# Hybrid encoder block on one core: the offset of the split gate and up weights inside their tiles varies from unit to unit

## Chip, cores and metric

The kernel runs on one core of one Trainium2 chip. The metric is the device time of one execution in microseconds; the time of a kernel is the median of its runs.

## What is computed

One layer of a bidirectional encoder with 512 tokens of width 2048: two token mixers side by side (global grouped-query attention, and attention in a 2-D neighbourhood), gated and summed, then a SwiGLU channel mixer with 5632 hidden features, all in float32. The change lies in the channel mixer's first half, the products with the gate and the up weights:

```python
h2 = rms_norm(x, norm2_w[l]) * (1.0 + sc2) + sh2
ff = (jax.nn.silu(h2 @ w_ffn_gate[l]) * (h2 @ w_ffn_up[l])) @ w_ffn_down[l]
x = x + g2 * ff
```

Here h2 is 512 x 2048, w_ffn_gate and w_ffn_up are 2048 x 5632, and w_ffn_down is 5632 x 2048.

## The kernel before

**Precision.** Every float32 operand is split into two float32r parts, hi (a copy rounded by ScalarE, ACT) and lo (source minus hi, by VectorE, DVE): `split` at line 117, with the ACT instruction at line 118 and the DVE instruction at line 119. A product is three matmuls into one PSUM bank: stationary hi with moving hi, stationary hi with moving lo, stationary lo with moving hi (`mm3` at line 125, the matmuls at lines 126, 127 and 128). So each matmul has its own weight load (LDWEIGHTS, PEld in the profile).

**Stages.** Until about 1100 us the kernel makes the modulation vectors, the input projection, both attentions and the merged output; there, and in the down projection at the end, a matmul mostly has 512 moving columns. `form2` (line 180) computes w_out and w_down with the weights as the moving operand. After w_out comes the gate and up stage, in two parts:

- Line 922 sets the offset `wbufs["at"]` to 16 elements. The first 512 columns of gate are computed directly (`block`, line 926) while the normalised activations h2 are still being made (transposes at line 839, tiles x, f, a and so on); it has 256 moving columns a matmul.
- The loop at line 975 then goes over 11 groups of 512 hidden features, gate and up in each; the first gate is already there, so 21 times it calls `group7` (line 796). This is a 7-product scheme for 2 x 2 blocks (Winograd's form of Strassen). `group7` takes 4 slices of 512 input features one after the other; one slice of one weight matrix, 512 x 512, is a *unit*. For each unit `wforms` (line 775) loads the weights in two transfers (line 133, from SP's queue), forms four differences on DVE (lines 785 to 788, into tiles ta and tb), and splits all into four pairs of tiles, whi and wlo.

**Order of work in a unit.** A unit has 7 products, in the order 1, 2, 3, 5, 6, 7, 4 (`ORDER`, line 756). Product 1 uses the first pair of tiles, products 2 and 3 the second, 5 and 6 the third, 7 and 4 the fourth. Each product has 2 x 2 blocks of 128 x 128 weights and each block has the three matmuls of `mm3`, so a unit has 84 matmuls, each with 128 x 128 weights as the stationary operand and 256 tokens as the moving one. After four units the seven banks are combined by one ACT and seven DVE instructions (lines 813 to 820), then SiLU (line 987) or the product of gate and up (line 990) follows, and the result goes to DRAM (line 991). At line 998 the offset goes back to 0 for the down projection.

**Tiles and addresses.** The split weights lie in rotating buffers, five for whi and five for wlo. Each buffer is 1024 + 64 elements wide, and the 1024 used elements begin at an offset inside it:

```python
def wtile(tag, at=None):
    at = wbufs["at"] if at is None else at
    return wp.tile([P, 1024 + wbufs["pad"]], F32R, tag=tag, name=tag, bufs=wbufs["w"])[:, at:at + 1024]
```

The buffers' width is 4352 bytes, 17 x 256. As the kernel's pools are laid out, a buffer begins on a multiple of 256 bytes in each partition, and a moving operand of this stage on a multiple of 1024. With the offset of 16 elements the weights of gate and up thus begin 64 bytes past a multiple of 256, and each block's 512-byte row of weights too. In the attention the weights and the moving operands both begin on multiples of 128 bytes.

Of the kernel before, what the change touches and what calls it, by code (L numbers as in the profile page):

```python
# [84 lines left out]
def encoder_block(ctx: ExitStack, tc, xp, c, w_ada, b_ada, norm1_w, w_in, q_norm_w, k_norm_w, tb,  # L85
# [12 lines left out]
    wbufs = {"raw": 4, "w": 4, "pad": 0, "at": 0}  # L98
# [4 lines that stand above are left out]
# [27 lines left out]
    def unit(w, k0, nk, c0, ncol):  # L130
        raw = wp.tile([P, 1024], F32, tag="raw", name="raw", bufs=wbufs["raw"])
        r3 = raw[:, :nk * ncol].rearrange("p (k n) -> p k n", k=nk)
        nc.sync.dma_start(r3, w[k0 * P:(k0 + nk) * P, c0:c0 + ncol].rearrange("(k p) n -> p k n", p=P))
        return raw[:, :nk * ncol], r3
# [628 lines left out]
    def half(t, n=2):  # L763
        return t.rearrange("p (a q n) -> p a q n", q=2, n=256) if n == 2 else t.rearrange("p (q n) -> p q n", q=2)

    def split7(parts, tiles, kinds):

        d = {}
        for (src, views), (hi, lo), rs in zip(parts, tiles, kinds):
            split(hi, lo, src)  # L770
            for r, v in zip(rs, views):
                d[r] = (v(hi), v(lo))
        return d

    def wforms(w, k0, c0):
        rt = []
        for a in range(2):
            raw, r3 = unit(w, k0 + 2 * a, 2, c0, 512)
            rt.append((raw, r3[:, :, :256], r3[:, :, 256:]))
        (_, b11, b12), (r1, b21, b22) = rt  # L780
        ta = wp.tile([P, 1024], F32, tag="ta", name="ta", bufs=2)
        tb = wp.tile([P, 1024], F32, tag="tb", name="tb", bufs=1)
        t1, t2_ = (half(ta)[:, a] for a in range(2))
        t3, t4 = (half(tb)[:, a] for a in range(2))
        V.tensor_sub(t1, b12, b11)  # L785
        V.tensor_sub(t2_, b22, t1)  # L786
        V.tensor_sub(t3, b22, b12)  # L787
        V.tensor_sub(t4, t2_, b21)
        hl = [[wtile(t) for t in ("whi", "wlo")] for _ in range(4)]
        col = lambda e: lambda t: t.rearrange("p (q n) -> p q n", q=2)[:, :, e * 256:(e + 1) * 256]  # L790
        blk = lambda e: lambda t: half(t)[:, e]
        g0 = [t[:, :512].rearrange("p (q n) -> p q n", q=2) for t in hl[0]]
        return split7(((b11, (lambda t: t,)), (r1, (col(0), col(1))), (ta, (blk(0), blk(1))), (tb, (blk(0), blk(1)))),
                      [g0] + hl[1:], HALVES[0])
# [180 lines left out]
    for n in range(FU):  # L975
        cs = []
        for w in (w_gate, w_up):
            c, v = c_tile()
            cs.append(c)
            if n == 0 and w is w_gate:  # L980
                for f in range(4):
                    S.activation(v[:, f // 2, :, f % 2], banks[f].rearrange("p (t n) -> p t n", t=2), AF.Silu)
                continue
            dst = (v[:, 0, 0], v[:, 1, 0]), (v[:, 0, 1], v[:, 1, 1])
            group7(lambda s: wforms(w, 4 * s, n * 512), hx, range(SU), dst)
            if w is w_gate:
                S.activation(c, c, AF.Silu)
        for a in range(2):
            sl = slice(a * 1024, (a + 1) * 1024)
            V.tensor_mul(cs[1][:, sl], cs[1][:, sl], cs[0][:, sl])  # L990
        (nc.sync if n < FU - 1 else nc.scalar).dma_start(ff_d[n], cs[1])
# [123 lines left out]
```

## Time and profile before

| what | value |
|---|---|
| median of three runs | 2671.52 us |
| the three runs | 2671.52, 2646.72, 2674.22 us |
| the profiled execution: its own time | 2649.24 us |
| its span, first to last instruction | 2647.4 us |
| mean granted TensorE clock | 0.994 |

The profile is of one execution. Its page gives the busy time of each engine: PE is TensorE's matmuls, PEld its weight loads, which overlap PE, DVE is VectorE, ACT is ScalarE, POOL is GpSimd, SP issues the transfers. A group of instructions is shown as line, engine, operation, output<-inputs, shapes, xcount | busy us, mean ns of one | idle time of the engine just before them and what ended it. The duration of a matmul is its time from start to end, and matmuls overlap: the pace is the distance from one start to the next. A row of the timeline has the start in us, the duration in us, the engine, the line and the instruction.

### The profile page before, as it was taken

What the parts mean: (1) busy time and instruction counts of PE and PEld (TensorE: products, weight loads), DVE (VectorE), ACT (ScalarE), POOL (GpSimd) and SP (SyncE); (2) the same over time, 40 slices, a digit from 0 to 9 for tenths busy, and PEclk for the clock granted to TensorE, in tenths of its full rate; (3) what the DMA queues carried; (4) which work ended last, traced back from release to release, by engine and by line L of the source; (5) the groups of instructions that cost most, each with busy time, mean ns of one, the idle gap of its engine ahead of it and who ended that gap; (6) DMA issues with size and microseconds to landing.
All of it is one profiled execution on the core that took longest, in us unless ns stands there. A gap on an engine that the chain in (4) does not pass through costs nothing.

```text
span 2647.4 us, 38740 instructions
## 1 busy us (share of the span) xinstructions
PE 2586.8 (98%) x15385; PEld 2276.6 (86%) x15385; DVE 1795.8 (68%) x2617; ACT 970.6 (37%) x1348; POOL 28.4 (1%) x38
## 2 busy tenths in 40 slices
PE   6999999999999999999999999999999999999997
PEld 5788777888888887788899999999999988888886
DVE  7994686555666566676688888888888863343227
ACT  5333344123233233323664444444444442232122
POOL 0000000000000000000000000000000000000000
PEclk9999999999999999999999999999999999999999
DMA  9873334655555687587344444443444374343332
GB/s 307 282 250 107 123 104 136 205 178 160 171 166 158 213 268 230 183 311 222 106 138 128 128 124 132 128 126 105 135 126 125 120 254 136 96 156 123 96 111 88
DMA packets 277158, 427.18 MB, mean 161 GB/s; under 512 B 17008, under 2 KB 140256, under 8 KB 274416
## 3 DMA queue, kind: packets, MB, share of 16 engines
q1 hardware_dynamic: 276640, 423.59, 50.4%
q8 instruction: 121, 1.98, 0.3%
q10 hardware_dynamic: 336, 1.11, 0.1%
q14 instruction: 61, 0.50, 0.1%
HBM read 392.11 MB, written 32.52 MB: 160 GB/s over the span
## 4 chain that ended last, share of the span: by engine, by line
PE 83%; DMA 7%; DVE 6%; ACT 2%; issue 1%; SPq 1%; DVEq 0%; ACTq 0%
PE mm L127 16%; PE mm L126 16%; PE mm L128 16%; PE S L126 6%; PE S L127 6%; PE S L128 6%; DMA raw<-in_w_ada 4%; PE Y L126 3%; PE Y L127 3%; PE Y L128 3%; DVE acc L266 2%; PE T L128 2%; PE T L126 1%; PE T L127 1%; DVE wlo L119 1%
## 5 line engine op out<-in xcount | busy, mean ns | idle before, releaser
L118 ACT ACTIVATE whi<-raw 128x1024 fp32r<-128x1024 f32 (+1 forms) x465 | 453.7, 978 | 974.5 <-PE mm L127 249.7
L119 DVE TENSOR_TENSOR wlo<-raw,whi 128x1024 fp32r<-128x1024 f32 (+1 forms) x465 | 520.1, 1121 | 406.6 <-ACT whi L118 402.5
L266 DVE SCALAR_TENSOR_TENSOR acc<-raw,cact,acc 128x512 f32<-128x512 f32 (+1 forms) x368 | 269.8, 740 | 127.4 <-DMA raw<-in_w_ada 121.9
L119 DVE TENSOR_TENSOR wlo<-ta,whi 128x1024 fp32r<-128x1024 f32 x84 | 102.7, 1223 | 67.2 <-ACT whi L118 67.1
L126 PE MATMUL S<-f,whi 128*128 128x256 f32 x504 | 139.1, 276 | 0.0
L127 PE MATMUL S<-f,whi 128*128 128x256 f32 x504 | 139.1, 276 | 0.0
L128 PE MATMUL S<-f,wlo 128*128 128x256 f32 x504 | 139.1, 276 | 0.0
L126 PE MATMUL mm<-f,whi 128*128 128x256 f32 x504 | 139.1, 276 | 0.0
L127 PE MATMUL mm<-f,whi 128*128 128x256 f32 x504 | 139.1, 276 | 0.0
L128 PE MATMUL mm<-f,wlo 128*128 128x256 f32 x504 | 139.1, 276 | 0.0
L118 ACT ACTIVATE whi<-ta 128x1024 fp32r<-128x1024 f32 x84 | 89.4, 1065 | 130.2 <-PE mm L127 127.8
L118 ACT ACTIVATE whi<-tb 128x1024 fp32r<-128x1024 f32 x84 | 89.7, 1067 | 125.1 <-PE S L127 122.8
L119 DVE TENSOR_TENSOR wlo<-tb,whi 128x1024 fp32r<-128x1024 f32 x84 | 102.5, 1220 | 5.8 <-ACT whi L118 3.1
L128 PEld LDWEIGHTS S<-f,wlo 128*128 128x128 f32 x504 | 94.6, 188 | 0.0
L127 PEld LDWEIGHTS mm<-f,whi 128*128 128x128 f32 x504 | 94.6, 188 | 0.0
L126 PEld LDWEIGHTS mm<-f,whi 128*128 128x128 f32 x504 | 94.6, 188 | 0.0
L126 PEld LDWEIGHTS S<-f,whi 128*128 128x128 f32 x504 | 94.6, 188 | 0.0
L127 PEld LDWEIGHTS S<-f,whi 128*128 128x128 f32 x504 | 94.6, 188 | 0.0
L128 PEld LDWEIGHTS mm<-f,wlo 128*128 128x128 f32 x504 | 94.6, 188 | 0.0
L786 DVE TENSOR_TENSOR ta<-raw,ta 128x512 f32<-128x512 f32 x84 | 58.0, 690 | 5.1 <-DMA raw<-in_w_up 2.3
L785 DVE TENSOR_TENSOR ta<-raw 128x512 f32<-128x512 f32 x84 | 57.9, 690 | 2.4
L787 DVE TENSOR_TENSOR tb<-raw 128x512 f32<-128x512 f32 x84 | 57.8, 688 | 1.8
(1894 smaller groups left out, 7628.3 us busy)
## 6 DMA issues: line engine op xcount, KB each, us to landing
raw<-in_w_in SPq DMA_DIRECT2D x133, 512.0 KB
raw<-in_w_ada SPq DMA_DIRECT2D x256, 256.0 KB
raw<-in_w_gate SPq DMA_DIRECT2D x88, 512.0 KB
raw<-in_w_up SPq DMA_DIRECT2D x88, 512.0 KB
raw<-in_w_down SPq DMA_DIRECT2D x88, 512.0 KB
raw<-in_w_ada SPq DMA_DIRECT2D x64, 512.0 KB
raw<-in_w_out SPq DMA_DIRECT2D x38, 512.0 KB
ffr<-ffd SPq DMA_DIRECT2D x22, 512.0 KB
```

Of the source, the lines that this page charges most:

```text
L118: S.activation(hi, src, AF.Copy)
L119: eng.tensor_sub(lo, src, hi)
L126: nc.tensor.matmul(o, lh, rh, start=start, stop=False, **kw)
L127: nc.tensor.matmul(o, lh, rl, start=False, stop=False, **kw)
L128: nc.tensor.matmul(o, ll, rh, start=False, stop=stop, **kw)
L266: V.scalar_tensor_tensor(acc, part, cact[:, k:k + 1], acc, op0=ALU.mult, op1=ALU.add)
L785: V.tensor_sub(t1, b12, b11)
L786: V.tensor_sub(t2_, b22, t1)
L787: V.tensor_sub(t3, b22, b12)
```

## The change

The offset, which is 16 elements (64 bytes) for all units of gate and up, is drawn from a cycle of four values at each call of `wforms`: 16, 19, 22 and 13 elements, 64, 76, 88 and 52 bytes. All eight weight tiles of a unit get the same offset. The width of the buffers stays as it is. The direct part with `block` comes before the first call and keeps 16; line 998 resets the offset to 0 as before, so the down projection is as it was.

```diff
+    offsets = itertools.cycle((16, 19, 22, 13))
+
     def wforms(w, k0, c0):
         rt = []
         for a in range(2):
...
         V.tensor_sub(t2_, b22, t1)
         V.tensor_sub(t3, b22, b12)
         V.tensor_sub(t4, t2_, b21)
+        wbufs["at"] = next(offsets)
         hl = [[wtile(t) for t in ("whi", "wlo")] for _ in range(4)]
```

## The prediction

> **What bounds the kernel now.** I read the head of the page first, then the stage table, then the waits inside the stage that the change touches, and last single matmuls.
>
> ```profile
> span 2647.4 us, 38740 instructions
> PE 2586.8 (98%) x15385; PEld 2276.6 (86%) x15385; DVE 1795.8 (68%) x2617; ACT 970.6 (37%) x1348; POOL 28.4 (1%) x38
> PE 83%; DMA 7%; DVE 6%; ACT 2%; issue 1%; SPq 1%; DVEq 0%; ACTq 0%
> ```
>
> The chain that ended last is TensorE for 83% of the span. The table by stages (columns: window, length, busy time and count of PE, PEld, DVE, ACT, POOL, granted clock, DMA share, GB/s) has the gate and up stage as its row from 1345 us:
>
> ```profile
> 0.00:300.00 300.00, 274.16 (x1237) 226.87 (x1238) 230.72 (x405) 114.24 (x206) 0.70 (x6) 0.99 0.71 229
> ...
> 1345.00:2144.00 799.00, 799.00 (x7053) 799.00 (x7052) 676.75 (x832) 352.96 (x373) 0.00 (x0) 1.00 0.40 125
> 2144.00:2200.00 56.00, 54.92 (x273) 46.35 (x272) 30.96 (x30) 20.53 (x20) 0.00 (x0) 1.00 0.87 312
> ```
>
> From 1345 to 2144 us TensorE is busy without a hole, at the full granted clock: 799.00 of 799.00 us with 7053 matmuls, 113.3 ns each. DVE works 676.75 us of it, ACT 352.96. In the waits of that stage no line has PE as the one that waits; the first and the last that matter are
>
> ```profile
> ACT whi L118 <- PE mm L127: 185.9, 166, 2.2
> ...
> DVE ta L786 <- DMA raw<-in_w_up: 2.3, 7, 0.6
> ```
>
> so ACT waits for TensorE to free a weight tile, and never the other way. The evacuation at line 813 comes once in each group of 336 matmuls:
>
> ```profile
> L813 ACT ACTIVATE p<-mm x21: 577/577/578, 1381.9 to 2143.2; 128x512 f32<-128x512 f32 x21
> ```
>
> (2143.2 - 1381.9) / 20 groups / 336 = 113.3 ns again, so the stage is paced by the matmul alone, from its first group to its last. What this pace consists of decides everything else. Four kinds of matmul show it (PE rows of the timeline; first column is the start):
>
> ```profile
> 2299.78 0.39 PE L127 MATMUL mm<-wlo,f7h 128*128 128x512 f32 x1
> ...
> 2302.95 0.39 PE L126 MATMUL mm<-whi,f7h 128*128 128x512 f32 x1
> ```
>
> These are 512 columns each, 14 of them from the first start to the last: 3.17 / 14 = 226.4 ns, twice the 113.3 ns of 256 columns. The pace follows the columns of the moving operand, though there is one weight load to 512 columns here and one to 256 there; 113.3 ns is the moving operand's own pace.
>
> ```profile
> 1299.10 0.28 PE L126 MATMUL mm<-x0h,whi 128*128 128x256 f32 x1
> ...
> 1304.63 0.28 PE L128 MATMUL mm<-x0h,wlo 128*128 128x256 f32 x1
> ```
>
> These are 256 columns with weights at the same 64 bytes, 47 steps in 5.53 us: 117.7 ns. So the same form has a second pace, 4.4 ns slower, and it lasts for dozens of matmuls without a wait. The groups of that stretch carry it in the mean duration of one, and show that it touches the loads too:
>
> ```profile
> L126 PE MATMUL mm<-x0h,whi 128*128 128x256 f32 x16 | 4.5, 281 | 0.0
> ...
> L127 PEld LDWEIGHTS mm<-x0l,whi 128*128 128x128 f32 x16 | 3.1, 192 | 0.0
> L128 PEld LDWEIGHTS mm<-x0h,wlo 128*128 128x128 f32 x16 | 3.0, 188 | 0.0
> ```
>
> 281 ns for the matmul there, against 276 in the whole gate and up stage:
>
> ```profile
> L126 PE MATMUL S<-f,whi 128*128 128x256 f32 x504 | 139.1, 276 | 0.0
> ```
>
> How it ends is to be seen after a break, at transposes:
>
> ```profile
> 1310.25 0.37 PE L126 MATMUL mm<-x1h,whi 128*128 128x256 f32 x1
> 1310.45 0.28 PE L127 MATMUL mm<-x1l,whi 128*128 128x256 f32 x1
> 1310.57 0.28 PE L128 MATMUL mm<-x1h,wlo 128*128 128x256 f32 x1
> 1310.69 0.28 PE L126 MATMUL mm<-x1h,whi 128*128 128x256 f32 x1
> 1310.80 0.28 PE L127 MATMUL mm<-x1l,whi 128*128 128x256 f32 x1
> ```
>
> Steps of 0.20, 0.12, 0.12, then 0.11: the fast pace. With constant alignment I find no change of pace inside an unbroken stream of 256-column matmuls; the big stage was entered fast and stayed fast to its end.
>
> **The change part by part.** It adds no instruction, removes none and moves none in any queue. It moves the start of eight weight tiles of every unit inside their buffers. A unit is 84 matmuls (7 products, 2 x 2 blocks, 3 matmuls each); 21 groups of 4 units make 84 units and 7056 matmuls and loads. Since 84 is a multiple of four, 21 units stand at each of 64, 76, 88 and 52 bytes; 63 units, 63 x 84 = 5292 loads, are displaced from today's 64. Moving operands, raw tiles and evacuations stay where they are.
>
> Moving operand: unchanged, 0 us. A gain below 113.3 ns is excluded, since the 512-column rows have the same pace per column with half the loads.
>
> Weight loads: how long one takes is seen where little else paces, in transposes of 128 columns:
>
> ```profile
> 1311.62 0.90 PEld L839 LDWEIGHTS S<-ident,x 128*128 128x128 f32 x8
> ```
>
> ```profile
> L839 PEld LDWEIGHTS S<-ident,x 128*128 128x128 f32 x32 | 3.6, 141 | 1.1 <-ACT h L842 0.5 <-ACT x L915 0.4
> ```
>
> Eight loads in 0.90 us, one of them 141 ns from start to end: (0.90 - 0.141) / 7 = 108 ns from load to load. Against 113.3 ns this leaves 5 ns. I take 0 for the displaced loads as long as one costs less than 5 ns more. No row has a weight load off a 64-byte grid, so the term is bounded: below by 0; above by the nearest slow rows, the 117.7 ns above (4.4 x 5292 = 23 us) and the attention's 256-column rows, whose weights lie on the same alignment as the moving operand:
>
> ```profile
> 333.46 0.28 PE L126 MATMUL Y<-pth,st 128*128 128x256 f32 x1
> ...
> 334.41 0.28 PE L128 MATMUL Y<-pth,st 128*128 128x256 f32 x1
> ```
>
> 8 steps in 0.95 us, 118.8 ns: 5.5 x 5292 = 29 us. I take 0, because today's stage is that same form at its fast pace and the moving operand sets it.
>
> [...]
>
> ACT and DVE write the displaced tiles (one of each per tile, 336 in all):
>
> ```profile
> L118 ACT ACTIVATE whi<-ta 128x1024 fp32r<-128x1024 f32 x84 | 89.4, 1065 | 130.2 <-PE mm L127 127.8
> L119 DVE TENSOR_TENSOR wlo<-tb,whi 128x1024 fp32r<-128x1024 f32 x84 | 102.5, 1220 | 5.8 <-ACT whi L118 3.1
> ```
>
> If misaligned writes cost more, the cover is DVE's 799.00 - 676.75 = 122 us of idle time, 0.36 us for each of 336 writes, almost a third of one; ACT has 446 us. The tiles come early as well:
>
> ```profile
> 1703.09 1.21 DVE L119 TENSOR_TENSOR wlo<-tb,whi 128x1024 fp32r<-128x1024 f32 x1
> 1703.09 0.19 PEld L126 LDWEIGHTS mm<-x1h,whi 128*128 128x128 f32 x1
> ```
>
> The fourth tile of a unit is being written as that unit's first load starts, and is needed 60 matmuls (6.8 us) later; 1.2 us are used. Cost 0; without the cover every 0.1 us per write would be 34 us.
>
> Sum: 0. Against the profiled execution's own 2649.24 us (span 2647.44 and 1.80 around it) that leaves 2649 us; I round to **2650**.
>
> **How this stands to the median.** The three runs are 2671.52, 2646.72 and 2674.22: two times about 26 us apart, the profiled execution with the lower. A whole stage at 117.7 instead of 113.3 ns would be 4.4 x 7056 = 31 us, so the upper pair looks like the stage at its slower pace for some 5900 of 7056 matmuls (26 / 4.4). That pace seems to hold on once a stream has it, every unit having the same alignment. Offsets that differ from unit to unit give it 83 occasions to fall out, and the fast pace has only the same 83 to be lost. As one of three loads is 4 ns longer in the slow rows, and the moving operand alone gives the fast pace, I expect the fast one to win. So I expect the low time of the two, 2650, 0.8% under the median.
>
> **The rivals.**
> 1. The offset doesn't do what it seems to, and the 26 us come from elsewhere, such as the w_ada transfers in the first 300 us, where PE has 26 us of idle time (300.00 - 274.16). For it: that row. Against it: the size fits the second pace. Then three runs of the new kernel scatter over the same two times, and the likelier median is the upper: 2672.
> 2. The changing offset draws the pace anew in every unit, and units fall in either. Half of them: 2649 + 31 / 2 = 2665; the 63 displaced alone: 2649 + 23 = 2672. For it: the same alignment shows both paces at 1299 and at 1345. Against: nothing changes pace inside the stage today.
> 3. Slower: loads from the displaced addresses become the bound. It decides once such a load costs over 5 ns more. Its price: the slow pace in every unit (31 us), and on it, in the displaced units, every load longer by the 4 ns that separate 192 from 188 in the slow rows: 4 x 5292 = 21 us; 2649 + 31 + 21 = 2701. For it: 5 ns is little, and the pace of 117.7 ns goes with longer loads. Against: in the fast rows 4 ns alone would be hidden. [...]
> 4. The writes of ACT or DVE slow by more than a third and DVE becomes the bound. Over 2700; nothing speaks for it.
>
> **How the numbers follow.** Forecast (2643 to 2656) 0.48; rival 1 0.22; rival 2 0.15; rival 3 0.12; rival 4 0.03. The range starts just under the lowest run, at 2642, and reaches to 2692, which takes in rivals 1 and 2 and the lighter half of rival 3 (one with 5.5 ns in all units is 2649 + 39 = 2688). One per cent, about what a measurement of this kernel can tell from no change, is 27 us: faster means under 2645, slower over 2698. The forecast lies 5 us above the first bound, so about a third of it, 0.16, falls below; rivals 3 and 4 are half over the upper, with a little for a heavier load, 0.10; within is the rest, 0.74.
>
> **What would show it.** In the changed profile: the group row of S<-f,whi with 276 ns again, line 813 at 38.07 us from group to group ((2143.2 - 1381.9) / 20), PE busy in the whole stage, DVE's and ACT's means at 1220 and 1065 ns within a few ns. Rival 1: a stage of the same length and a median near 2672. Rival 2: 276 and 281 ns mixed, by unit. Rival 3: 282 or more in the displaced units and loads over 188 ns. Rival 4: waits of PE for wlo at line 119. I am wrong if the stage's pace is over 114 ns, or if a stage at 113.3 comes with a median over 2660.

## The result and the profile after

| kernel | runs | median | lowest to highest |
|---|---|---|---|
| before | 22 | 2673.10 us | 2642.65 to 2683.91 |
| after | 22 | 2645.07 us | 2637.34 to 2650.44 |

The ratio of after to before is 0.9944, with a 95% interval of 0.9916 to 0.9972: a little faster, by less than 1%. The two medians are 28 us (1.0%) apart, more than that ratio says, because the median of before falls among its high runs. The lists of runs say more than the medians. The kernel before has two times: 9 of the 22 runs lie between 2642.65 and 2649.59 us (the low time, mean 2645.7), 13 between 2671.52 and 2683.91 (the high time, mean 2676.7), none in between; the means are 31 us apart. All 22 runs of the changed kernel lie at the low time, mean 2645.3. The change makes the good case no faster. It removes the bad one.

The profile after is therefore almost that of before, which had the low time. Its page, then the stage's row in the table by stages:

```profile
span 2647.3 us, 38740 instructions
PE 2586.2 (98%) x15385; PEld 2277.2 (86%) x15385; DVE 1795.7 (68%) x2617; ACT 970.3 (37%) x1348; POOL 26.5 (1%) x38
```

```profile
1345.00:2144.00 799.00, 799.00 (x7047) 799.00 (x7046) 676.61 (x831) 352.05 (x372) 0.00 (x0) 1.00 0.39 125
```

The window has 7047 matmuls where before had 7053, and DVE and ACT are as before. The writes into displaced tiles cost nothing that shows (1220 and 1065 ns before):

```profile
L118 ACT ACTIVATE whi<-ta 128x1024 fp32r<-128x1024 f32 x84 | 89.4, 1065 | 130.3 <-PE mm L127 127.9
...
L119 DVE TENSOR_TENSOR wlo<-tb,whi 128x1024 fp32r<-128x1024 f32 x84 | 102.7, 1222 | 6.2 <-ACT whi L118 3.1
```

The six matmuls that after lacks in the window lead to its most telling rows. This execution came into the stage at the slow pace and kept it until 1361 us; in 16 us at 117.8 ns fit five or six matmuls fewer than at 113.3. Its first unit, at 64 bytes, and its second, at 76, in the groups of their two windows (1351.3 to 1361 us, and 1361.6 to 1370.7):

```profile
L126 PE MATMUL S<-f,whi 128*128 128x256 f32 x8 | 2.2, 281 | 0.0
```

```profile
L126 PE MATMUL S<-f,whi 128*128 128x256 f32 x8 | 2.2, 276 | 0.0
```

And the place where one becomes the other, in the timeline; the second unit begins with the third row:

```profile
1360.92 0.28 PE L127 MATMUL Y<-f0a,whi 128*128 128x256 f32 x1
1361.04 0.28 PE L128 MATMUL Y<-f0a,wlo 128*128 128x256 f32 x1
1361.16 0.28 PE L126 MATMUL mm<-x1h,whi 128*128 128x256 f32 x1
1361.28 0.28 PE L127 MATMUL mm<-x1l,whi 128*128 128x256 f32 x1
1361.40 0.28 PE L128 MATMUL mm<-x1h,wlo 128*128 128x256 f32 x1
1361.51 0.28 PE L126 MATMUL mm<-x1h,whi 128*128 128x256 f32 x1
1361.62 0.28 PE L127 MATMUL mm<-x1l,whi 128*128 128x256 f32 x1
```

Steps of 0.12 up to 1361.40, 0.11 from there on, without a break or a wait. From start to start, the first unit takes 117.8 ns a matmul, the second 113.4, and all others 113.3, those at 64 bytes too. So the evacuation of line 813, now at 816, comes at the 38.07 us from group to group that the prediction named as its sign, (2143.9 - 1382.6) / 20:

```profile
L816 ACT ACTIVATE p<-mm x21: 578/578/580, 1382.6 to 2143.9; 128x512 f32<-128x512 f32 x21
```

### The profile page after: what moved, and what is told of

It is laid out like the page before. It is cut to its first block, busy times and chain, and to the rows that moved or that the text cites. A ratio compares the mean times of both kernels' runs of the same rounds, so it can differ in the third digit from the quotient of the medians.

```text
span 2647.3 us, 38740 instructions
## 1 busy us (share of the span) xinstructions
PE 2586.2 (98%) x15385; PEld 2277.2 (86%) x15385; DVE 1795.7 (68%) x2617; ACT 970.3 (37%) x1348; POOL 26.5 (1%) x38
## 4 chain that ended last, share of the span: by engine, by line
PE 81%; DMA 9%; DVE 6%; ACT 2%; issue 1%; SPq 1%; DVEq 0%; ACTq 0%
PE mm L127 16%; PE mm L126 16%; PE mm L128 16%; PE S L126 6%; PE S L127 6%; PE S L128 6%; DMA raw<-in_w_ada 5%; PE Y L126 3%; PE Y L127 3%; PE Y L128 3%; DVE acc L266 2%; DVE wlo L119 1%; PE T L128 1%; PE T L126 1%; PE T L127 1%
## 5 line engine op out<-in xcount | busy, mean ns | idle before, releaser
L118 ACT ACTIVATE whi<-ta 128x1024 fp32r<-128x1024 f32 x84 | 89.4, 1065 | 130.3 <-PE mm L127 127.9
L119 DVE TENSOR_TENSOR wlo<-tb,whi 128x1024 fp32r<-128x1024 f32 x84 | 102.7, 1222 | 6.2 <-ACT whi L118 3.1
```

Source lines behind the costliest of these rows:

```text
L118: S.activation(hi, src, AF.Copy)
L119: eng.tensor_sub(lo, src, hi)
```

## The experiments

Theory A: the high time is the gate and up stage at the slower of two matmul paces, and a displaced unit takes a stream out of it. Rivals: B, the 31 us arise elsewhere; C, displaced loads cost time by themselves; and within A, whether it is the variation from unit to unit that cures, or the displacement, or certain addresses. In the experiments' runs the kernel before kept its two times: with the 22 above it ran 90 times, 53 times between 2642.65 and 2656.82 us and 37 times between 2671.52 and 2686.91.

**The high time, seen.** The kernel before, three times more for its profile.

> The kernel before, unchanged, for one more profile. Theory A (two paces of the gate and up matmul): if this execution has the high time (2671 to 2684 us), its gate and up stage shows 117.7 ns from start to start and 281 ns for one matmul, line 813 comes every 39.6 us instead of 38.07, and the rest of the kernel is as before; if it has the low time (2643 to 2650 us), all is as in the first profile. Theory B (the 31 us come from elsewhere, such as the transfers of the first 300 us): with the high time the gate and up stage is 38.07 us a group as ever and another stage is 31 us longer.

> The kernel before once more, for a profile of its high time. If it comes: 117.8 ns and 281 ns a matmul in the whole gate and up stage, as in the units 1 to 83 behind a first unit at offset 0, and the other stages as in the first profile.

> As the run before it: another draw of the kernel before, with the same expectation.

Measured: 2652.19, 2648.86 and 2684.22 us. The first two are low and have 113.3 ns in every unit. The third is the high time. Its span is 2682.4 us, 35.0 over the first profile's. Line 813, the stage's row, and groups of it:

```profile
L813 ACT ACTIVATE p<-mm x21: 577/583/586, 1386.8 to 2177.8; 128x512 f32<-128x512 f32 x21
```

```profile
1345.00:2144.00 799.00, 799.00 (x6786) 799.00 (x6785) 656.32 (x809) 336.82 (x358) 0.00 (x0) 1.00 0.40 122
```

```profile
L126 PE MATMUL S<-f,whi 128*128 128x256 f32 x480 | 134.9, 281 | 0.0
```

```profile
L126 PEld LDWEIGHTS S<-f,whi 128*128 128x128 f32 x480 | 92.2, 192 | 0.0
```

(2177.8 - 1386.8) / 20 / 336 = 117.7 ns, at a granted clock of 1.00, with PE busy throughout and DVE less busy than before: TensorE itself is slower, nothing keeps it waiting. 84 units x 84 x 4.4 ns = 31 us of the 35; the rest lies ahead of the stage, which begins 3.7 us later than in the first profile (in the first of these three, a low run, it began 2.7 us later). The first two rows of the table by stages, with the w_ada transfers, are those of the first profile within 3 us of PE time:

```profile
0.00:300.00 300.00, 273.29 (x1236) 226.45 (x1237) 230.61 (x404) 114.26 (x206) 0.70 (x6) 0.99 0.71 229
300.00:1290.00 990.00, 973.72 (x4515) 798.48 (x4513) 627.75 (x1047) 332.11 (x549) 27.13 (x32) 0.99 0.58 186
```

The second row in the first profile:

```profile
300.00:1290.00 990.00, 971.35 (x4516) 796.12 (x4514) 629.94 (x1048) 335.37 (x554) 27.69 (x32) 0.99 0.59 186
```

B falls.

**Displaced without variation.**

```diff
-    offsets = itertools.cycle((16, 19, 22, 13))
+    offsets = itertools.cycle((19,))
```

> All units at 19 elements, 76 bytes: displaced as three quarters of the change's units are, but the same in every unit. Theory A with variation as the cure: two times again, about 2645 and 2676 us, as in the kernel before. Theory A with displacement as the cure (an address off the 64-byte grid shifts a load's reads against the moving operand's): 2645 us in all runs. Theory C (displaced loads cost time): over 2650 in all runs.

Measured: 12 runs, 2643.91 to 2651.61, median 2649.42; ratio 0.9945 (0.9903 to 0.9986). Beside them before had 14 low runs (mean 2649.6) and 9 high (mean 2682.7). The profile of this kernel came into the stage at the slow pace (117.8 ns in the direct part) and has 113.4 ns in the first unit, 113.3 in all others. So 76 bytes throughout does what the change does: variation is not the cure, and C falls at 76 bytes.

**Variation without the displaced addresses.**

```diff
-    offsets = itertools.cycle((16, 19, 22, 13))
+    offsets = itertools.cycle((16, 20, 24, 12))
```

> The offset goes round 64, 80, 96 and 48 bytes, all multiples of 16: it varies from unit to unit as in the change, but no load leaves the grid of 16 bytes. If variation is the cure: 2645 us in all runs. If being off the 16-byte grid is: two times, 2645 and 2676 us.

Measured: neither. All 12 runs lie from 2672.31 to 2681.63, median 2674.87, ratio 1.0072 (1.0036 to 1.0108).

```profile
L816 ACT ACTIVATE p<-mm x21: 577/582/582, 1382.3 to 2169.2; 128x512 f32<-128x512 f32 x21
```

(2169.2 - 1382.3) / 20 / 336 = 117.1 ns a matmul. From unit border to unit border it goes by the offset, the same in every round: 113.4 at 64 bytes, 118.8 at 80, 118.7 at 96, 117.8 at 48. In this run each offset has a pace of its own, and three of these four multiples of 16 bytes are slow.

**No displacement at all.**

```diff
-    offsets = itertools.cycle((16, 19, 22, 13))
+    offsets = itertools.cycle((0,))
```

> All units at offset 0, weights on the same alignment as the moving operand, as in the attention. If the distance of 64 bytes matters: the pace is that of the attention's rows, 118.8 ns, and the time 2645 + 39 = 2684 us in all runs. If it does not: two times, 2645 and 2676 us, as in the kernel before.

Measured: six runs, 2693.18 to 2699.31, median 2695.30, ratio 1.0130 (1.0072 to 1.0187), one time and not two.

```profile
L816 ACT ACTIVATE p<-mm x21: 580/581/582, 1381.8 to 2187.7; 128x512 f32<-128x512 f32 x21
```

(2187.7 - 1381.8) / 20 / 336 = 119.9 ns: each matmul takes 120.0, a little more than the attention's rows of 118.8 had said. Groups from 1400 to 2000 us, matmuls and loads:

```profile
L126 PE MATMUL mm<-f,whi 128*128 128x256 f32 x360 | 101.9, 283 | 0.0
```

```profile
L126 PEld LDWEIGHTS mm<-f,whi 128*128 128x128 f32 x360 | 69.1, 192 | 0.0
```

**One unit displaced.** Only the first unit at 76 bytes, and then only unit 42, all others at 64:

```diff
-    offsets = itertools.cycle((16, 19, 22, 13))
+    offsets = itertools.chain((19,), itertools.repeat(16))
```

```diff
-    offsets = itertools.cycle((16, 19, 22, 13))
+    offsets = itertools.chain((16,) * 42, (19,), itertools.repeat(16))
```

> Only the first of the 84 units is at 76 bytes, all others at 64 as before. Theory A as the second profile shows it (at 64 bytes a stream keeps whichever of two paces it came with, at 76 it goes to the fast one): 2645 us in all runs, and 113.3 ns in the whole stage. If the displacement has to be there all the time: two times, 2645 and 2676 us.

> Only unit 42, in the middle, is at 76 bytes. Theory A: the units before it at either pace, the units after it at the fast one; two times again, but half as far apart, 2645 and about 2660 us (42 units x 84 x 4.4 ns = 15.5 us).

Measured: with the first unit, 12 runs from 2644.21 to 2651.59, median 2648.73, ratio 0.9958 (0.9922 to 0.9995); before had 8 high runs of 29 beside them (mean 2682.2). Its profile came in slow, as a group of the direct part just ahead of the stage shows (1335.2 to 1346.5 us), has 113.4 ns in the first unit and 113.3 in all others ((2138.8 - 1377.5) / 20 / 336):

```profile
L128 PE MATMUL mm<-xh,wlo 128*128 128x256 f32 x16 | 4.5, 281 | 0.0
```

```profile
L816 ACT ACTIVATE p<-mm x21: 577/577/577, 1377.5 to 2138.8; 128x512 f32<-128x512 f32 x21
```

With unit 42, ten runs from 2642.35 to 2653.70, and two at 2661.14 and 2663.73, 13 and 16 us above the median of the ten (2647.9), as expected; the ratio, 0.9965 (0.9924 to 1.0005), tells nothing apart. Its profile was of a low run that came in fast, so the change of pace at unit 42 itself was not seen. From the first unit's run: 64 bytes keeps the fast pace for 83 units once a single unit has given it.

**One unit at offset 0.**

```diff
-    offsets = itertools.cycle((16, 19, 22, 13))
+    offsets = itertools.chain((0,), itertools.repeat(16))
```

> Only the first unit is at offset 0, at its own slow pace of 120.0 ns; the others at 64. If 64 bytes keep the pace that a stream comes with: 117.8 ns in all the other units and 2676 us in all runs. If a stream at 64 bytes goes fast when it comes out of any other offset, as out of 48 in the cycle of 16-byte steps: 2645 us in all runs. If it is chance: two times.

Measured: 10 runs, 2677.60 to 2694.19, median 2679.19, ratio 1.0086 (1.0042 to 1.0129): none low. Its profile came into the stage at the fast pace (the direct part, 1334.4 to 1347.9 us), had 120.0 ns in the first unit, and the groups behind that (1368 to 2170 us) show why no run is low:

```profile
L128 PE MATMUL mm<-xh,wlo 128*128 128x256 f32 x16 | 4.4, 276 | 0.0
```

```profile
L128 PE MATMUL S<-f,wlo 128*128 128x256 f32 x488 | 137.3, 281 | 0.0
```

That is 117.8 ns in each of the 83 units: 64 bytes keeps the slow pace just as long. With this, the run with the first unit at 76 bytes and the third profile of before, the two times are explained: one and the same program, with one of two paces in the whole stage, according to how the stream began.

**All offsets in one profile.**

```diff
-    offsets = itertools.cycle((16, 19, 22, 13))
+    offsets = itertools.cycle(range(64))
```

> The offset goes up by 4 bytes from one unit to the next, from 0 to 252 bytes, and begins again at 0 for the last 20 units: one profile with the pace of every offset. From what is known: 120.0 ns at 0, 117.8 at 48, 118.8 at 80, 118.7 at 96, 113.3 at 52, 64, 76 and 88. If it is the grid of 16 bytes that decides, all multiples of 16 but 64 are slow and all others fast; if it is the distance to the moving operand's 128 bytes, the slow ones lie round 0 and 128.

Measured: 2679.46 us. The time from a unit's first matmul to the next unit's, by 84, read like this for 76 bytes (unit 19) and 108 bytes (unit 27):

```profile
1535.92 0.28 PE L126 MATMUL mm<-xh,whi 128*128 128x256 f32 x1
...
1545.44 0.28 PE L126 MATMUL mm<-x0h,whi 128*128 128x256 f32 x1
...
1614.98 0.28 PE L126 MATMUL mm<-xh,whi 128*128 128x256 f32 x1
...
1625.25 0.28 PE L126 MATMUL mm<-x0h,whi 128*128 128x256 f32 x1
```

9.52 / 84 = 113.3 ns and 10.27 / 84 = 122.3. All 64 (upper line bytes, lower line ns):

```
    0     4     8    12    16    20    24    28    32    36    40    44    48    52    56    60
120.0 118.3 115.8 116.6 118.3 116.8 118.7 116.7 118.4 119.9 119.2 117.8 117.8 113.7 117.8 119.6
   64    68    72    76    80    84    88    92    96   100   104   108   112   116   120   124
113.5 118.4 118.3 113.4 118.9 120.0 113.6 118.3 117.3 119.8 119.9 122.3 120.0 118.3 119.4 118.7
  128   132   136   140   144   148   152   156   160   164   168   172   176   180   184   188
118.6 118.6 118.0 116.7 120.0 116.7 117.8 119.8 120.0 117.7 120.0 118.8 118.1 118.2 117.8 118.2
  192   196   200   204   208   212   216   220   224   228   232   236   240   244   248   252
113.4 117.7 116.7 120.0 116.7 117.3 119.9 120.7 116.6 120.0 117.7 119.8 117.3 119.8 117.6 120.1
```

Five of 64 have the pace of 113.3 ns but for a few matmuls at the unit's start: 52, 64, 76, 88 and 192 bytes. The change uses exactly the first four. Neither of the two rules in the expectation holds: 56, 60, 68 and 72 bytes, between 52, 64 and 76, have 117.8 to 119.6 ns, multiples of 16 and others alike. That 52, 64, 76 and 88 lie 12 bytes apart is a fact of this table; what makes them good stays open. Nothing is under 113.3 ns. Nearly every offset was seen behind one neighbour only, and a number of the table need not be the only pace of its offset: 64 bytes has two, and 96, expected at 118.7 as in the cycle of 16-byte steps (where it stood behind 80 bytes), has 117.3 here, behind 92. Coming out of a slow neighbour (48, 60, 72, 84, 188), all five went fast, mostly within the first product; 64 did so out of 48 and 60, and not out of 0.

Nor do all the slow offsets go with longer loads. At 204 bytes (1854 to 1863 us) a matmul takes 120.0 ns, and its loads are as short as in the fast stream, 188 ns:

```profile
L126 PEld LDWEIGHTS mm<-xh,whi 128*128 128x128 f32 x7 | 1.3, 188 | 0.0
```

```profile
L127 PE MATMUL mm<-xl,whi 128*128 128x256 f32 x8 | 2.3, 282 | 0.0
```

**Address or distance?** All weights at 108 bytes, and the tiles of the left side of the memory 32 bytes further on; in the first three units of a group the moving operands then begin 32 bytes past a multiple of 256, in the fourth at a multiple. (The fourth unit's moving operands begin on a multiple of 256 in every kernel here, not of 1024 as the others do in the kernel before; the distances below count modulo 256 bytes.)

```diff
-    const.tile([P, 32], F32, name="left_edge")
+    const.tile([P, 40], F32, name="left_edge")
...
-    offsets = itertools.cycle((16, 19, 22, 13))
+    offsets = itertools.cycle((27,))
```

> All weights at 108 bytes, the slowest offset of the sweep (122.3 ns), and the tiles of the left side of the memory, the moving operands of three of a group's four units among them, 32 bytes further on; the fourth unit's moving operands stay. If the distance between weights and moving operand decides, the first three units of a group are at a distance of 76 bytes and at 113.3 ns, and the fourth is at 108 and about 122 ns. If the address of the weights alone decides: 122 ns in all four.

Measured: 2694.67 us, with another stretch ahead of the stage longer too (its first matmul is 17 us later than in the first profile; that was not followed up). The stage: 113.8, 113.3, 113.3 and 122.1 ns in the four units of every group. A third and a fourth unit by their groups (1543.2 to 1551.5 us, 1552.6 to 1562 us):

```profile
L126 PE MATMUL mm<-f,whi 128*128 128x256 f32 x8 | 2.2, 276 | 0.0
```

```profile
L128 PE MATMUL mm<-xh,wlo 128*128 128x256 f32 x8 | 2.3, 287 | 0.0
L127 PE MATMUL mm<-xl,whi 128*128 128x256 f32 x7 | 2.0, 287 | 0.0
L126 PE MATMUL mm<-xh,whi 128*128 128x256 f32 x7 | 2.0, 284 | 0.0
```

The same weight address, 9 ns apart, by the place of the moving operand. Nor is a moving operand at the new place fast by itself. The direct part of this run has its weights at 64 bytes as ever (line 922) and its first moving operands 32 bytes further on, a distance of 32:

```profile
1315.50 0.28 PE L126 MATMUL mm<-x0h,whi 128*128 128x256 f32 x1
...
1321.06 0.28 PE L128 MATMUL mm<-x0h,wlo 128*128 128x256 f32 x1
```

47 steps in 5.56 us, 118.3 ns, where the sweep has 118.4 for 32 bytes. It is the distance between the two that decides. Why it does is not shown.

**76 bytes in the direct part too.**

```diff
-    wbufs["at"] = 16
+    wbufs["at"] = 19
```

This is the kernel before with line 922 changed alone.

> All weights of the gate and up stage at 76 bytes, those of the direct part before the first group too, in which some 350 matmuls ran at 117.7 ns at 64 bytes. If 76 bytes is fast there too: one time in all runs, 1 to 2 us under that of the low runs of the kernel before, too little to be told apart; the profile's matmuls of the direct part have 276 ns instead of 281.

Measured: 12 runs from 2641.57 to 2652.98, median 2649.13, ratio 0.9937 (0.9896 to 0.9978). In the direct part the long slow stretch is gone; the group from 1299 to 1307.5 us had 281 ns before:

```profile
L126 PE MATMUL mm<-x0h,whi 128*128 128x256 f32 x16 | 4.4, 277 | 0.0
```

Short slow stretches are left, behind breaks in the stream: 11 matmuls from 1307.4 us have 120.0 ns from start to start. The "350 matmuls" of the expectation were too many: in the first profile of before about 150 of the direct part's 384 ran at the slow pace, in the third about 280. As expected, the gain, 1.2 us by the larger count, can't be told apart in the time. One number in place of a cycle is all that the kernel needs.

## Why the prediction was right, and where its reasons were not

**The sum of 0** held: span 2647.3 against 2647.4 us, stage, writes of ACT and DVE, and cover as reckoned. Each had its row except the 0 for the displaced loads, for which the prediction found none; the floor of 113.3 ns stands in all 64 offsets.

**The two times.** Dividing 26 us by 4.4 ns gave 5900 matmuls; with more runs the distance is 31 us, the whole stage of 7056, and the third profile of before shows it in every unit. Here the step "the upper pair looks like the stage at its slower pace" was right, and its size was a matter of two runs against one.

**The forecast of the low time** came true in 22 of 22 runs, as did the way of it: the profile after falls out of the slow pace in its first displaced unit.

**The reason given for it was only half right.** The prediction let varying offsets "give it 83 occasions to fall out" and expected the fast pace to win because the moving operand alone sets it. Varying is not what helps: one constant offset of 76 bytes does the same, one unit suffices, and a cycle of four other offsets is slow in all runs. Nor is the fast pace favoured in general: 59 of 64 offsets are slow in the sweep. The step that failed is the 0 for the displaced loads, taken "because today's stage is that same form at its fast pace": tacitly, a displaced offset is like 64 or better. That held at 52, 76 and 88 bytes; at 48, 80 and 96 the same form took 117.8 to 118.8 ns. Nor is a load that outgrows 5 ns what decides, as the prediction had it: at 204 bytes the pace was 120.0 ns with loads of 188. The prediction was lucky in the addresses.

**The bounds** were too narrow above: 4.4 and 5.5 ns from the nearest rows, where the sweep has up to 9.0 (122.3). With that in the displaced units, 9.0 x 5292 = 48 us, the time would have been 2697, over the range.

**The rivals.** 1 fell by the third profile of before. 2, units at either pace: not with these offsets. The cycle of 16-byte steps comes near its price, with the displaced units slow (2674.87 against 2672), but draws nothing: each offset has its pace again in every round. 3, loads from the displaced addresses as the bound: the 2695.30 of offset 0 is near its price of 2701, with loads of 192 ns and matmuls of 120.0, but its mechanism fell: loads from one and the same address went with 113.3 and with 122.1 ns, and 120.0 ns came with loads of 188. 4 fell with DVE at 1222 ns and no wait of PE.

**Open** is what makes five distances good, and what decides at which pace a stream at 64 bytes begins: the low time in 53 of 90 runs, by chance as far as these runs show. Where it is decided can be seen. In the twelve profiles whose direct part is at a distance of 64 bytes, the stage begins at the pace that the matmuls took up behind the direct part's last transposes, some 16 us ahead of it: seven times the fast one, five times the slow one. Earlier in the direct part one execution has both, one after the other, with breaks in the stream between them.

## What to carry to other kernels

When a kernel has two times and its profile shows the bounding engine busy throughout at full clock, compare the mean duration and the start-to-start distance of its instructions in both: here 276 against 281 ns for one, and 113.3 against 117.8 from start to start, was the whole of it. Where each matmul of 256 moving columns has a weight load, as here (113.3 to 122.3 ns over 64 distances), the distance between the two addresses is a parameter to sweep, and a sweep with another offset in each unit takes a single profile, though it shows most offsets behind one neighbour only. Settle it by many runs: an offset that keeps whichever pace it is given looks good or bad by chance, as 64 bytes does here (the low time in 53 of 90 runs).

## What the runs showed of the hardware

- With 256 moving columns, the pace of a matmul depends on the distance in memory between the weights loaded and the moving operand: 113.3 to 122.3 ns over distances of 0 to 252 bytes (modulo 256) in steps of 4, five of 64 at 113.3 as the sweep passed them. Weights at one address (108 bytes) ran at 122.1 ns, and at 113.3 with a moving operand 32 bytes further on.
- At one distance (64 bytes) both 113.3 and 117.8 ns last for thousands of matmuls without change. A single unit at another distance sets either: 76 bytes the fast one, 0 the slow one.
- The duration of the loads is no sure sign of the pace. At 113.3 ns they last 188; at 64 bytes and 117.8 ns one of three lasts 192, at 0 bytes and 120.0 ns all do, but at 204 bytes and 120.0 ns those of line 126 last 188 again.
